# Chunk states and carried parts of a bidirectional scan as plain fp32 products, with the states in two buffers

## The chip, the cores and the metric

The kernel runs on one core of one Trainium2 chip. The metric is the device time of one execution in microseconds (us). Before the change three runs gave 1725.57 us as their median, between 1724.66 and 1726.45 us.

The engines have short names here: PE multiplies matrices (PEld is its loading of the stationary operand, which overlaps it), DVE is the vector engine, ACT the scalar engine, POOL is GpSimd, and SP issues most of the transfers (DMAs).

## What is computed

The kernel is one encoder layer over 1024 tokens of width 1024: a projection, a bidirectional state-space scan beside a neighbourhood attention, an output projection and an MLP. All inputs and outputs are fp32. The change touches the scan alone. For each direction it runs over 8 chunks of 128 tokens and 2 groups of 8 heads:

```python
    cb = jnp.einsum("bclgn,bcsgn->bclsg", cc, bc)
    y_diag = jnp.einsum("bclsge,bcsgep->bclgep", cb[..., None] * decay, xc)
    decay_to_end = jnp.exp(a_cum[:, :, -1:] - a_cum)
    chunk_states = jnp.einsum("bclgn,bclgep->bcgepn", bc, xc * decay_to_end[..., None])
    chunk_decay = jnp.exp(a_cum[:, :, -1])

    def step(h, inp):
        s_c, d_c = inp
        return d_c[..., None, None] * h + s_c, h
    ...
    _, h_in = lax.scan(step, h0, (jnp.moveaxis(chunk_states, 1, 0), jnp.moveaxis(chunk_decay, 1, 0)))
    h_in = jnp.moveaxis(h_in, 0, 1)
    y_off = jnp.einsum("bclgn,bcgepn->bclgep", cc, h_in) * jnp.exp(a_cum)[..., None]
    return (y_diag + y_off).reshape(bsz, t, SSM_GROUPS, HEADS_PER_GROUP, SSM_HEAD_DIM)
```

`chunk_states` (what a chunk adds to the state) and `y_off` (what the state carried into a chunk adds to its output) are the two products that are changed.

## The kernel before

**Split operands.** Nearly every large product of the kernel is made of fp32 operands split in two: a high part, the operand rounded to the type fp32r (an ACT copy), and a low part, the operand less its high part (a subtraction on DVE or POOL). The helper `mm3` (L178 to L180) issues three products of fp32r operands into one PSUM tile: high by high, high by low, low by high. The trace shows a product by its line in the helper and its tile.

**Stages.** The first part normalises and transposes the input, makes the scan's inputs (`xbc`, `conv`, `decays`) and the gate (`pz`). The scan follows (`backward` and `forward`, one chunk and one head group at a time, the two directions running against each other). Beside the scan runs the projection to q, k and v (`qkv_proj`, tiles `pq`, 1152 products), which needs nothing of the scan and fills PE between its steps. Then come the attention with the output projection, and the MLP.

**The scan's step.** For a direction d, a chunk c and a group g:

- `backward` multiplies B by C (tile `pcb`, L587), builds a 128x128 matrix for each head (`rb`: two POOL subtractions at L612, a DVE select at L618, an ACT exponential, a DVE product at L625), and multiplies each with the inputs `xs` (tile `pd`, L630, eight small products).
- `carried` makes the carried part: C is split (`ch` on ACT, L562; `cl` on DVE, L563), three products with the split state go to tile `py`, and a DVE product at L567 makes `yo` of it, which POOL adds to the output (`y1`, L641 or L666); DVE then adds `pd` (L642).
- `decay_state` makes the next state: POOL scales the inputs (`xw`, L653 or L672), `xw` is split (`xh` on ACT, L540; `xl` on DVE, L541), three products with the split B (`bNh`, `bNl`) go to tile `pS`. POOL multiplies the old state by its decay in place (`st`, L549), DVE adds `pS` (L550), and the new state is split (`sh` on ACT, L553; `sl` on DVE, L554) for the next `carried`. The first state of each direction and group is a DVE copy (L546).

There are 28 calls of `carried` and 28 of `decay_state`. The tiles `pcb`, `pS` and `py` share two PSUM buffers (tag "s"), so each has to wait until the last reader of the one two before it is done. B is split after a transpose in `conv`, four times (L184, L185).

**What sets the order.** The program is written once, step by step; a scheduler of the build then orders the instructions of each engine by its own estimate of the times, and each engine runs its list strictly in that order. A wait at the head of a list holds up everything behind it.

Of the kernel before, what the change touches and what calls it, by code (L numbers as in the profile page):

```python
# [9 lines left out]
F32 = mybir.dt.float32  # L10
F32R = mybir.dt.float32r
BF16 = mybir.dt.bfloat16
I32 = mybir.dt.int32
AF = mybir.ActivationFunctionType
# [4 lines left out]
P = 128  # L19
T = 1024  # L20
D = 1024
NT = T // P
# [33 lines left out]
def hymba_block(  # L56
# [25 lines left out]
    nc = tc.nc  # L82
    mul, add, sub = ALU.mult, ALU.add, ALU.subtract
# [25 lines left out]
    def ps_tp(name="tp"):  # L109
        return ps.tile([P, 512], F32, tag="tp", name=name, bufs=2)  # L110

    def ps_s(name="s"):
        return ps.tile([P, 512], F32, tag="s", name=name, bufs=2)
# [63 lines left out]
    def mm3(pt, ah, al, bh, bl, first, last):  # L177
        nc.tensor.matmul(pt, lhsT=ah, rhs=bh, start=first, stop=False)  # L178
        nc.tensor.matmul(pt, lhsT=ah, rhs=bl, start=False, stop=False)  # L179
        return nc.tensor.matmul(pt, lhsT=al, rhs=bh, start=False, stop=last)  # L180

    def split_from_psum(hi, lo, src, scalar=None):
        if scalar is None:
            nc.scalar.activation(hi, src, AF.Copy)  # L184
            nc.vector.tensor_tensor(lo, src, hi.bitcast(F32), op=sub)  # L185
        else:
            nc.scalar.activation(hi, src, AF.Copy, scale=scalar)
            nc.vector.scalar_tensor_tensor(
                lo, src, scalar, hi.bitcast(F32), op0=mul, op1=sub
            )  # L190
# [28 lines left out]
    with ExitStack() as ph:  # L219
# [4 lines left out]
        sp = ph.enter_context(tc.tile_pool(name="sp", bufs=1, side="right"))  # L224
        bT = sp.tile([P, 2, T], F32, name="bT")
        cT = sp.tile([P, 2, T], F32, name="cT")
        bNh = sp.tile([P, NT, 2, P], F32R, name="bNh")
        bNl = sp.tile([P, NT, 2, P], F32R, name="bNl")
        acum = sp.tile([P, 2, NT, 16], F32, name="acum")
        c1 = sp.tile([P, 2, NT, 16], F32, name="c1")  # L230
        e1 = sp.tile([P, 2, NT, 16], F32, name="e1")
# [6 lines left out]
        with ExitStack() as p0:  # L238
# [12 lines left out]
            for t in range(NT):  # L251
# [4 lines left out]
                for h in range(2):  # L256
                    s = slice(h * 512, (h + 1) * 512)
# [19 lines left out]
            for h in range(2):  # L277
                s = slice(4 * h, 4 * h + 4)
# [32 lines left out]
        with ExitStack() as p1:  # L311
            qp = p1.enter_context(tc.tile_pool(name="qp", bufs=2, side="right", reuse_waits="tile"))

            rrow = qp.tile([P, T], F32, name="rrow", bufs=1)
            for h in range(2):
# [5 lines left out]
                    op=mul,  # L321
# [127 lines left out]
            def conv(ft, ub):  # L449
                def tap(k):  # L450
                    return pcol[:, k * 12 + ft : k * 12 + ft + 1]

                acc = qp.tile([P, T], F32, tag="acc", name="acc")
                nc.scalar.activation(
                    acc,
                    ub[:, 0:T],
                    AF.Identity,
                    bias=pcol[:, 60 + ft : 61 + ft],
                    scale=tap(0),
                )  # L460
                for k in range(1, 5):
                    nc.vector.scalar_tensor_tensor(
                        acc, ub[:, k : k + T], tap(k), acc, op0=mul, op1=add
                    )
                dst = acc if ft < 8 else (bT, cT)[(ft - 8) // 2][:, ft % 2, :]
                nc.scalar.activation(dst, acc, AF.Silu)
                if ft >= 10:
                    return
                xn = qp.tile([P, NT, P], F32, tag="xn", name="xn") if ft < 8 else None
                for g in range(2):  # L470
                    pt = ps_tp("ptx")
                    for j in range(4):
                        c = 4 * g + j
                        nc.tensor.transpose(
                            pt[:, j * P : (j + 1) * P],
                            dst[:, c * P : (c + 1) * P],
                            ident,
                        )
                    pv = pt.rearrange("p (j f) -> p j f", j=4)
                    if ft < 8:  # L480
                        nc.scalar.copy(xn[:, 4 * g : 4 * g + 4, :], pv)
                    else:
                        s = (slice(None), slice(4 * g, 4 * g + 4), ft - 8)
                        split_from_psum(bNh[s], bNl[s], pv)
                if ft < 8:
                    nc.sync.dma_start(
                        xs_dr[:, :, ft * P : (ft + 1) * P].rearrange("c p f -> p c f"),
                        xn,
                    )
# [11 lines left out]
            for g in range(2):  # L501
                get = load_w_nat(w_in[0], 0, KD, OFF_Z + 512 * g, nc.vector)
                for t in range(NT):
                    pt = ps_mm("pz")
                    for k in range(KD):
                        s = (slice(None), k, slice(t * P, (t + 1) * P))
# [5 lines left out]
        def hb(v):  # L512
            return v.unsqueeze(2).broadcast_to([P, 8, HD])

        def h8(v):
            return v.rearrange("p (e d) -> p e d", d=HD)

        with ExitStack() as p2:
            qp = p2.enter_context(tc.tile_pool(name="qs", bufs=2, side="right", reuse_waits="tile"))
# [13 lines left out]
            st = [[None, None], [None, None]]  # L533

            def decay_state(d, c, g, xw):
                prev = st[d][g]
                pS = ps_s("pS")
                xh = qp.tile([P, 512], F32R, tag="xh", name="xh", bufs=1)
                xl = qp.tile([P, 512], F32R, tag="xl", name="xl", bufs=1)
                nc.scalar.activation(xh, xw, AF.Copy)  # L540
                nc.vector.tensor_tensor(xl, xw, xh.bitcast(F32), op=sub)  # L541
                mm3(pS, bNh[:, c, g, :], bNl[:, c, g, :], xh, xl, True, True)
                new = prev and prev[0]
                if prev is None:
                    new = qp.tile([P, 512], F32, tag=f"st{d}{g}", name="st", bufs=1)
                    nc.vector.tensor_copy(new, pS)  # L546
                else:
                    dec = ed[:, d, c, 8 * g : 8 * g + 8]
                    nc.gpsimd.tensor_tensor(h8(new), h8(new), hb(dec), op=mul)  # L549
                    nc.vector.tensor_tensor(new, new, pS, op=add)  # L550
                sh = qp.tile([P, 512], F32R, tag=f"sh{g}", name="sh", bufs=1)
                sl = qp.tile([P, 512], F32R, tag=f"sl{g}", name="sl", bufs=1)
                nc.scalar.activation(sh, new, AF.Copy)  # L553
                nc.vector.tensor_tensor(sl, new, sh.bitcast(F32), op=sub)  # L554
                st[d][g] = (new, sh, sl)

            def carried(d, c, g):
                py = ps_s("py")
                ct = cT[:, g, c * P : (c + 1) * P]
                ch = qp.tile([P, P], F32R, tag="ch", name="ch", bufs=2)  # L560
                cl = qp.tile([P, P], F32R, tag="cl", name="cl", bufs=2)
                nc.scalar.activation(ch, ct, AF.Copy)  # L562
                nc.vector.tensor_tensor(cl, ct, ch.bitcast(F32), op=sub)  # L563
                mm3(py, ch, cl, *st[d][g][1:], True, True)
                yo = qp.tile([P, 512], F32, tag="yo", name="yo", bufs=1)
                e = e1[:, d, c, 8 * g : 8 * g + 8]
                nc.vector.tensor_tensor(h8(yo), h8(py), hb(e), op=mul)  # L567
                return yo
# [12 lines left out]
            def backward(c, g):  # L581
# [57 lines left out]
                if c < NT - 1:  # L639
                    yo = carried(1, c, g)  # L640
                    nc.gpsimd.tensor_tensor(y1, y1, yo, op=add)  # L641
# [9 lines left out]
                if c > 0:  # L651
                    xw = qp.tile([P, 512], F32, tag="xw", name="xw", bufs=1)
                    nc.gpsimd.tensor_tensor(h8(xw), h8(xs), hb(wd[:, 1, c, hs]), op=mul)  # L653
                    decay_state(1, c, g, xw)
# [55 lines left out]
            for g in range(2):  # L710
                ps4 = slice(4 * g, 4 * g + 4)
                for b, pt, rt in qkv_proj(OFF_Q, g):
                    hl = normed_split(pt, rt, pcol[:, 80:81])
                    s = slice(b * P, (b + 1) * P)
# [58 lines left out]
    with ExitStack() as ph:  # L773
# [292 lines left out]
        for t in (0, 4, 1, 5, 2, 6, 3, 7):  # L1066
            xt = x2[:, t, :]
            for h, get in enumerate((get0, get1)):
                pt = ps_mm("po")
                s = slice(t * P, (t + 1) * P)  # L1070
# [3 lines left out]
                d = xt[:, h * 512 : (h + 1) * 512]  # L1074
# [173 lines left out]
    with ExitStack() as ph:  # L1248
# [32 lines left out]
        for fb in range(4):  # L1281
# [18 lines left out]
            for i in ORD:  # L1300
# [14 lines left out]
                for t in range(4):  # L1315
                    pt = (X if i in (1, 6, 7, 4) else Y)[t]
                    ts = slice(t * P, t * P + P)
                    for u in range(2):
                        (ah, al), (wh, wl) = wa[u]
                        for a in range(2):  # L1320
                            s = slice(a * 512 + t * P, a * 512 + t * P + P)
                            d = slice(a * 512, a * 512 + 512)
# [6 lines left out]
                    d = acc[:, tt, dh * 512 : (dh + 1) * 512]  # L1329
# [47 lines left out]
```

## Time and profile before

| what | value |
|---|---|
| median of three runs | 1725.57 us (1724.66 to 1726.45) |
| the profiled execution's own time | 1725.33 us |
| its span, from the first to the last instruction | 1723.5 us |
| granted PE clock, mean | 0.98 |
| DVE, ACT and POOL, share of the span | 64%, 42%, 41% |
| matrix and vector instructions that are recorded | 20879 |

The profile comes from one execution. An engine's busy time is that of its own instructions, without waits. Products on PE are pipelined: a record lasts longer than the distance to the next one's start, so that a busy PE isn't a PE at its peak, and a product that is held up shows as a longer record. A plain fp32 product is recorded as two instructions with one weight load each. "Idle before, releaser" tells what the engine waited for, as inferred from semaphores. Times in a view are us from the span's start unless marked ns.

### The profile page before, as it was taken

What the parts mean: (1) busy time and instruction counts of PE and PEld (TensorE: products, weight loads), DVE (VectorE), ACT (ScalarE), POOL (GpSimd) and SP (SyncE); (2) the same over time, 40 slices, a digit from 0 to 9 for tenths busy, and PEclk for the clock granted to TensorE, in tenths of its full rate; (3) what the DMA queues carried; (4) which work ended last, traced back from release to release, by engine and by line L of the source; (5) the groups of instructions that cost most, each with busy time, mean ns of one, the idle gap of its engine ahead of it and who ended that gap; (6) DMA issues with size and microseconds to landing.
All of it is one profiled execution on the core that took longest, in us unless ns stands there. A gap on an engine that the chain in (4) does not pass through costs nothing. (4 is left out here: it accounts for less than half of the span.)

```text
span 1723.5 us, 20879 instructions
## 1 busy us (share of the span) xinstructions
PE 1636.0 (95%) x7461; PEld 1304.6 (76%) x7461; DVE 1106.3 (64%) x1687; ACT 726.5 (42%) x1189; POOL 705.6 (41%) x496
## 2 busy tenths in 40 slices
PE   6999999989888999999999988999999978999999
PEld 5788888777766777777767767788888866888887
DVE  5767214889787744778787776454343359787863
ACT  5434223434344434555565533454444443333330
POOL 4000004888778741221242242244444426555551
PEclk9999999999998999999999999999999989999999
DMA  8213338876675796754453141254344394644231
GB/s 200 62 37 104 89 98 242 210 195 207 213 206 161 234 311 199 240 150 138 132 183 123 56 159 49 73 190 153 134 159 147 125 349 149 201 141 166 92 110 73
DMA packets 178499, 269.75 MB, mean 157 GB/s; under 512 B 13963, under 2 KB 105051, under 8 KB 178395
## 3 DMA queue, kind: packets, MB, share of 16 engines
q1 hardware_dynamic: 135419, 231.18, 42.6%
q10 hardware_dynamic: 42976, 37.23, 7.1%
q8 instruction: 59, 0.97, 0.2%
q14 instruction: 45, 0.37, 0.1%
HBM read 185.21 MB, written 86.50 MB: 158 GB/s over the span
## 5 line engine op out<-in xcount | busy, mean ns | idle before, releaser
L760 POOL TENSOR_TENSOR wl<-wraw,wh 128x1024 fp32r<-128x1024 f32 x110 | 300.1, 2740 | 350.1 <-ACT wh L759 336.7
L745 PE MATMUL px<-wh,ahl 128*128 128x512 f32 x512 | 163.7, 397 | 9.8 <-ACT ahl L759 9.8
L759 ACT ACTIVATE wh<-wraw 128x1024 fp32r<-128x1024 f32 x110 | 115.7, 1054 | 127.4 <-issue 42.4
L179 PE MATMUL pq<-wl,hTh 128*128 128x512 f32 x384 | 153.1, 400 | 4.6 <-DVE wl L149 4.4
L745 PE MATMUL px<-h,wh 128*128 128x512 f32 x496 | 156.5, 396 | 0.0
L178 PE MATMUL pq<-wh,hTh 128*128 128x512 f32 x384 | 153.1, 401 | 1.9 <-ACT wh L148 1.2
L180 PE MATMUL pq<-wh,hTl 128*128 128x512 f32 x384 | 151.9, 396 | 0.0
L759 ACT ACTIVATE ahl<-ar 128x1024 fp32r<-128x1024 f32 x56 | 58.9, 1053 | 173.0 <-PE px L745 89.6
L760 DVE TENSOR_TENSOR ahl<-ar,ahl 128x1024 fp32r<-128x1024 f32 x56 | 107.3, 1917 | 37.4 <-ACT ahl L759 36.2
L745 PEld LDWEIGHTS px<-wh,ahl 128*128 128x128 f32 x512 | 97.3, 190 | 31.9 <-ACT ahl L759 10.2
L745 PEld LDWEIGHTS px<-h,wh 128*128 128x128 f32 x496 | 93.4, 189 | 22.4
L149 DVE TENSOR_TENSOR wl<-wraw,wh 128x1024 fp32r<-128x1024 f32 x40 | 55.0, 1376 | 83.3 <-ACT wh L148 82.7
L878 POOL TENSOR_TENSOR mb<-braw,nam 128x256 f32<-128x256 f32 (+1 forms) x48 | 41.0, 884 | 159.7 <-DVE nmx L936 123.4
L184 ACT ACTIVATE pth<-ptp 128x384 fp32r<-128x384 f32 (+1 forms) x128 | 58.4, 459 | 107.8 <-PE ptp L959 106.8
L745 PE MATMUL px<-wl,ahl 128*128 128x512 f32 x256 | 100.9, 394 | 0.0
L745 PE MATMUL px<-h,wl 128*128 128x512 f32 x248 | 98.1, 396 | 0.0
L179 PEld LDWEIGHTS pq<-wl,hTh 128*128 128x128 f32 x384 | 73.2, 191 | 22.1 <-DVE wl L149 7.9
L149 POOL TENSOR_TENSOR wl<-wraw,wh 128x1024 fp32r<-128x1024 f32 x18 | 43.8, 2446 | 110.5 <-ACT wh L148 84.3
L745 PE MATMUL pz<-wh,ahl 128*128 128x512 f32 x256 | 82.8, 400 | 6.5 <-DVE acc L1330 5.0
L178 PEld LDWEIGHTS pq<-wh,hTh 128*128 128x128 f32 x384 | 72.9, 190 | 18.2 <-ACT wh L148 2.5
L180 PEld LDWEIGHTS pq<-wh,hTl 128*128 128x128 f32 x384 | 73.2, 191 | 14.7
L612 POOL TENSOR_TENSOR rb<-rb,c 128x512 f32<-128x512 f32 x64 | 75.0, 1192 | 21.5 <-DMA rb<-cum_dr 18.7
(265 smaller groups left out, 4242.6 us busy)
## 6 DMA issues: line engine op xcount, KB each, us to landing
act_dr<-cq SPq DMA_DIRECT2D x56, 512.0 KB, 3.0
ar<-act_dr SPq DMA_DIRECT2D x56, 512.0 KB, 3.8
wraw<-in_w_in_dram SPq DMA_DIRECT2D x44, 512.0 KB, 4.0
rb<-cum_dr SPq DMA_DIRECT2D x32, 512.0 KB, 7.6
wraw<-in_w_mlp_in_dram SPq DMA_DIRECT2D x32, 512.0 KB, 4.7
wraw<-in_w_mlp_out_dram SPq DMA_DIRECT2D x32, 512.0 KB, 5.3
q_dr<-hl ACTq DMA_DIRECT2D x64, 128.0 KB, 3.2
k_dr<-hl ACTq DMA_DIRECT2D x16, 512.0 KB, 3.2
```

The costliest lines, as they stand in the source:

```text
L149: lo_eng.tensor_tensor(lo[:, 0:n], raw[:, 0:n], hi[:, 0:n].bitcast(F32), op=sub)
L178: nc.tensor.matmul(pt, lhsT=ah, rhs=bh, start=first, stop=False)
L179: nc.tensor.matmul(pt, lhsT=ah, rhs=bl, start=False, stop=False)
L180: return nc.tensor.matmul(pt, lhsT=al, rhs=bh, start=False, stop=last)
L184: nc.scalar.activation(hi, src, AF.Copy)
L612: nc.gpsimd.tensor_tensor(rb[:, d], rb[:, d], c1[:, d, c, h0 : h0 + 4].unsqueeze(2).broadcast_to([P, 4, P]), op=sub,)
L745: nc.tensor.matmul(pt, lhsT=a, rhs=b, start=f, stop=l, skip_group_check=True)
L759: nc.scalar.activation(hl[0], src, AF.Copy)
L760: eng.tensor_tensor(hl[1], src, hl[0].bitcast(F32), op=sub)
L878: nc.gpsimd.tensor_tensor(mb[:, s].rearrange("p (s r c) -> p s r c", r=16, c=8), v[:, a:b], nam[:, s].rearrange("p (s r c) -> p s r c", r= ...
```

## The change

The two products of a scan step become one plain fp32 product each, so that nothing of `xw`, of the state, of C and of B has to be split. B is kept once as fp32 (`bN`, four ACT copies in place of four splits). The state gets two buffers for each direction and group: POOL reads the old one and writes its decayed copy into the other, where DVE adds `pS`. The first state's copy moves from DVE to ACT.

```diff
@@ -224,8 +224,7 @@
         sp = ph.enter_context(tc.tile_pool(name="sp", bufs=1, side="right"))
         bT = sp.tile([P, 2, T], F32, name="bT")
         cT = sp.tile([P, 2, T], F32, name="cT")
-        bNh = sp.tile([P, NT, 2, P], F32R, name="bNh")
-        bNl = sp.tile([P, NT, 2, P], F32R, name="bNl")
+        bN = sp.tile([P, NT, 2, P], F32, name="bN")
         acum = sp.tile([P, 2, NT, 16], F32, name="acum")
         c1 = sp.tile([P, 2, NT, 16], F32, name="c1")
         e1 = sp.tile([P, 2, NT, 16], F32, name="e1")
@@ -481,7 +480,7 @@
                         nc.scalar.copy(xn[:, 4 * g : 4 * g + 4, :], pv)
                     else:
                         s = (slice(None), slice(4 * g, 4 * g + 4), ft - 8)
-                        split_from_psum(bNh[s], bNl[s], pv)
+                        nc.scalar.copy(bN[s], pv)
                 if ft < 8:
                     nc.sync.dma_start(
                         xs_dr[:, :, ft * P : (ft + 1) * P].rearrange("c p f -> p c f"),
@@ -535,33 +534,20 @@
             def decay_state(d, c, g, xw):
                 prev = st[d][g]
                 pS = ps_s("pS")
-                xh = qp.tile([P, 512], F32R, tag="xh", name="xh", bufs=1)
-                xl = qp.tile([P, 512], F32R, tag="xl", name="xl", bufs=1)
-                nc.scalar.activation(xh, xw, AF.Copy)
-                nc.vector.tensor_tensor(xl, xw, xh.bitcast(F32), op=sub)
-                mm3(pS, bNh[:, c, g, :], bNl[:, c, g, :], xh, xl, True, True)
-                new = prev and prev[0]
+                nc.tensor.matmul(pS, lhsT=bN[:, c, g, :], rhs=xw, start=True, stop=True)
+                new = qp.tile([P, 512], F32, tag=f"st{d}{g}", name="st", bufs=2)
                 if prev is None:
-                    new = qp.tile([P, 512], F32, tag=f"st{d}{g}", name="st", bufs=1)
-                    nc.vector.tensor_copy(new, pS)
+                    nc.scalar.copy(new, pS)
                 else:
                     dec = ed[:, d, c, 8 * g : 8 * g + 8]
-                    nc.gpsimd.tensor_tensor(h8(new), h8(new), hb(dec), op=mul)
+                    nc.gpsimd.tensor_tensor(h8(new), h8(prev), hb(dec), op=mul)
                     nc.vector.tensor_tensor(new, new, pS, op=add)
-                sh = qp.tile([P, 512], F32R, tag=f"sh{g}", name="sh", bufs=1)
-                sl = qp.tile([P, 512], F32R, tag=f"sl{g}", name="sl", bufs=1)
-                nc.scalar.activation(sh, new, AF.Copy)
-                nc.vector.tensor_tensor(sl, new, sh.bitcast(F32), op=sub)
-                st[d][g] = (new, sh, sl)
+                st[d][g] = new
 
             def carried(d, c, g):
                 py = ps_s("py")
                 ct = cT[:, g, c * P : (c + 1) * P]
-                ch = qp.tile([P, P], F32R, tag="ch", name="ch", bufs=2)
-                cl = qp.tile([P, P], F32R, tag="cl", name="cl", bufs=2)
-                nc.scalar.activation(ch, ct, AF.Copy)
-                nc.vector.tensor_tensor(cl, ct, ch.bitcast(F32), op=sub)
-                mm3(py, ch, cl, *st[d][g][1:], True, True)
+                nc.tensor.matmul(py, lhsT=ct, rhs=st[d][g], start=True, stop=True)
                 yo = qp.tile([P, 512], F32, tag="yo", name="yo", bufs=1)
                 e = e1[:, d, c, 8 * g : 8 * g + 8]
                 nc.vector.tensor_tensor(h8(yo), h8(py), hb(e), op=mul)
```

The order of all engines is planned anew. On PE, in the first half of the scan, this is a step where a chunk's small products, the state's products and the next carried part stand in a row before:

```order
L179 MATMUL pq<-wl,hTh 128x512
L630 MATMUL pd<-xs,rb 128x64 x8
L178 MATMUL pS<-xh,bNh 128x512
L179 MATMUL pS<-xl,bNh 128x512
L180 MATMUL pS<-xh,bNl 128x512
L178 MATMUL py<-sh,ch 128x512
L179 MATMUL py<-sl,ch 128x512
L180 MATMUL py<-sh,cl 128x512
L705 MATMUL ptq<-ident,qn 128x128 x8
L180 MATMUL pq<-wh,hTl 128x512
```

And the same step in the changed program:

```order
L180 MATMUL pq<-wh,hTl 128x512
L616 MATMUL pd<-xs,rb 128x64 x8
L537 MATMUL pS<-xw,bN 128x512
L550 MATMUL py<-st,cT 128x512
L691 MATMUL ptq<-ident,qn 128x128 x8
L178 MATMUL pq<-wh,hTh 128x512
```

Six products have become two, and the neighbours are the same: `pS` still stands right behind `pd`, and `py` right behind `pS`, ahead of eight transposes (`ptq`) and the next projection products.

On DVE, at the step that adds to the output tile `y_2522`, there stands before (`qn` and `hl` belong to the projection, `rb` to the next chunk's matrices):

```order
L567 TENSOR_TENSOR yo<-py,e_100 128x512
L563 TENSOR_TENSOR cl<-cT,ch 128x128
L554 TENSOR_TENSOR sl<-st,sh 128x512
L699 SCALAR_TENSOR_TENSOR qn<-pq,rcol,rq 128x512
L550 TENSOR_TENSOR st<-st,pS 128x512
L541 TENSOR_TENSOR xl<-xw,xh 128x512
L642 TENSOR_TENSOR y_2522<-y_2522,pd 128x512
L188 SCALAR_TENSOR_TENSOR hl<-ptq,pcol,hl 128x512
L618 COPY_PREDICATED rb<-lmask,rb 128x512
L567 TENSOR_TENSOR yo<-py,e_100 128x512
L563 TENSOR_TENSOR cl<-cT,ch 128x128
L554 TENSOR_TENSOR sl<-st,sh 128x512
```

And at the same step of the changed program, where the output tile is called `y_2327`:

```order
L553 TENSOR_TENSOR yo<-py,e_99 128x512
L149 TENSOR_TENSOR wl<-wraw,wh 128x1024
L685 SCALAR_TENSOR_TENSOR qn<-pq,rcol,rq 128x512
L544 TENSOR_TENSOR st<-st,pS 128x512
L188 SCALAR_TENSOR_TENSOR hl<-ptq,pcol,hl 128x512
L628 TENSOR_TENSOR y_2327<-y_2327,pd 128x512
L604 COPY_PREDICATED rb<-lmask,rb 128x512
L553 TENSOR_TENSOR yo<-py,e_99 128x512
```

The five splits (`cl`, `sl`, `xl`, `cl`, `sl`) are gone, and the last subtraction of a weight split (`wl`) has moved from ahead of `yo` to behind it. The rest stands in the same order.

On POOL, around the same step, there stands before (`rq` belongs to the projection):

```order
L638 TENSOR_TENSOR y_2522<-xs,cf 128x512
L672 TENSOR_TENSOR xw<-xs,wd 128x512
L201 TENSOR_SCALAR rq<-sq 128x8
L202 TENSOR_TENSOR rq<-rq,half 128x8
L641 TENSOR_TENSOR y_2522<-y_2522,yo 128x512
L549 TENSOR_TENSOR st<-st,ed 128x512
L612 TENSOR_TENSOR rb<-rb,c_99 128x512 x2
L653 TENSOR_TENSOR xw<-xs,wd 128x512
```

And in the changed program:

```order
L624 TENSOR_TENSOR y_2327<-xs,cf 128x512
L201 TENSOR_SCALAR rq<-sq 128x8
L202 TENSOR_TENSOR rq<-rq,half 128x8
L627 TENSOR_TENSOR y_2327<-y_2327,yo 128x512
L598 TENSOR_TENSOR rb<-rb,c_98 128x512 x2
L658 TENSOR_TENSOR xw<-xs,wd 128x512
L543 TENSOR_TENSOR st<-st,ed 128x512
```

The forward direction's scaling of the inputs (`xw`, L672 before and L658 now) has moved from ahead of the addition of `yo` to behind it and behind two subtractions on `rb`, and the decay of its state (`st`) stands right behind it. (L653 is the backward direction's `xw`.) The work is the same.

## The prediction

> **What bounds the kernel now.** I read the page's busy times first, then the busy time by stage, then PE's waits in the stage of the scan.
>
> ```profile
> span 1723.5 us, 20879 instructions
> PE 1636.0 (95%) x7461; PEld 1304.6 (76%) x7461; DVE 1106.3 (64%) x1687; ACT 726.5 (42%) x1189; POOL 705.6 (41%) x496
> ...
> core 0: us, PE busy (x) PEld busy (x) DVE busy (x) ACT busy (x) POOL busy (x), PEclk, DMA share, GB/s
> ...
> 268.80:604.00 335.20, 302.81 (x1450) 242.29 (x1449) 264.52 (x388) 134.59 (x241) 262.83 (x242) 0.98 0.74 213
> 604.00:670.00 66.00, 65.34 (x297) 52.84 (x297) 25.03 (x32) 20.64 (x30) 20.33 (x22) 1.00 0.77 250
> ```
>
> PE is the busiest engine by far, so a change is worth what it does to PE: to its work, and to its waits. The change lies in the second row by stage, 268.8 to 604, where the scan runs beside the projection; there DVE (264.5 of 335.2) and POOL (262.8) are nearly as busy as PE. From 604 to 670 the rest of the projection runs alone.
>
> A busy PE hides stalls, since a product that is held up is a longer record. So I count PE's work over 268.8 to 670, which holds the whole projection and the whole scan.
>
> ```profile
> L179 PE MATMUL pq<-wl,hTh 128*128 128x512 f32 x384 | 153.1, 400 | 4.6 <-DVE wl L149 4.4
> L178 PE MATMUL pq<-wh,hTh 128*128 128x512 f32 x384 | 153.1, 401 | 1.9 <-ACT wh L148 1.2 <-DVE hl L188 0.6
> L180 PE MATMUL pq<-wh,hTl 128*128 128x512 f32 x384 | 151.9, 396 | 0.0
> ...
> 609.94 0.39 PE L179 MATMUL pq<-wl,hTh 128*128 128x512 f32 x1
> 610.17 0.39 PE L180 MATMUL pq<-wh,hTl 128*128 128x512 f32 x1
> 610.39 0.39 PE L178 MATMUL pq<-wh,hTh 128*128 128x512 f32 x1
> 610.62 0.39 PE L179 MATMUL pq<-wl,hTh 128*128 128x512 f32 x1
> ...
> L178 PE MATMUL pS<-xh,bNh 128*128 128x512 f32 x28 | 12.3, 441 | 1.7 <-ACT rb L623 1.0 <-ACT xh L540 0.7
> L178 PE MATMUL py<-sh,ch 128*128 128x512 f32 x28 | 12.7, 455 | 3.8 <-DVE yo L567 2.5 <-DVE st L550 1.3
> L630 PE MATMUL pd<-xs,rb 128*128 128x64 f32 x256 | 32.3, 274 | 8.2 <-DVE rb L625 7.3 <-issue 0.9
> L587 PE MATMUL pcb<-cT,bT 128*128 128x128 f32 x32 | 7.2, 310 | 8.6 <-DVE yo L567 7.5 <-DVE st L550 1.1
> L705 PE MATMUL ptq<-ident,qn 128*128 128x128 f32 x128 | 21.4, 280 | 2.7 <-DVE qn L699 1.8 <-ACT sz L576 0.8
> ...
> 435.65 1.89 PE L630 MATMUL pd<-xs,rb 128*128 128x64 f32 x16
> 418.82 0.60 PE L705 MATMUL ptq<-ident,qn 128*128 128x128 f32 x4
> ```
>
> Where nothing holds it up, a product of split operands starts 0.227 us after the one before (three steps from 609.94 to 610.62). The 3 x 384 products of the projection take 1152 x 0.227 = 261.5 us, and `pS` and `py` with three lines of 28 each 168 x 0.227 = 38.1. Sixteen records of `pd` take 1.89 us, the last with its 0.27 us of length, so they stand (1.89 - 0.27)/15 = 0.108 apart: 256 of them 27.6 us. Four transposes take 0.60 with a last one of 0.28, so 0.107 apart: 128 of them 13.7, and the 32 records of `pcb`, of the same size, 3.4. The sum is 344.3 us of work in 401.2 us. **About 57 us are lost to waits**, and these are what the change can win back.
>
> ```profile
> PE pcb L587 <- DVE yo L567: 7.5, 4, 3.1
> PE pd L630 <- DVE rb L625: 7.3, 9, 1.3
> PE pq L179 <- DVE wl L149: 4.4, 5, 1.7
> PE py L178 <- DVE yo L567: 2.5, 2, 2.0
> PE ptq L705 <- DVE qn L699: 1.8, 5, 0.9
> PE py L179 <- DVE sl L554: 1.6, 2, 1.2
> PE py L178 <- DVE st L550: 1.3, 4, 0.5
> ```
>
> These are PE's waits in that stage (total, times, longest). The rows name DVE for 26.4 us, and the two stage rows leave PE (335.2 - 302.8) + (66.0 - 65.3) = 33.1 us idle, so DVE is named for 80%. Only `sl` among them is removed. The others are instructions that stay, but that come late because DVE runs its list in order and is busy 79% of the stage.
>
> **The change part by part.** First the product itself: 28 `pS` and 28 `py` of three products each become one plain fp32 product each. The trace has the same shape once, in the first part, on operands that were not split.
>
> ```profile
> 47.97 0.40 PE L180 MATMUL px<-hTh,wl 128*128 128x512 f32 x1
> 48.20 1.02 PE L324 MATMUL prr<-dg,cst 128*128 128x512 f32 x2
> 48.66 0.80 PE L178 MATMUL px<-hTh,wh 128*128 128x512 f32 x1
> 49.30 0.39 PE L179 MATMUL px<-hTl,wh 128*128 128x512 f32 x1
> ```
>
> The product `prr` is recorded as two. It starts at 48.20; the product behind it is held up (0.80 instead of 0.39 long), and the next but one starts at 49.30. Less one step of 0.227 for the product between, `prr` takes 49.30 - 0.23 - 48.20 = 0.87 us, against 3 x 0.227 = 0.68 of the three that it replaces. **PE's work grows by 0.19 x 56 = 10.7 us.** In a stream without waits this comes out whole; it is covered only where PE would have waited anyway.
>
> Then the splits that go:
>
> ```profile
> L554 DVE TENSOR_TENSOR sl<-st,sh 128x512 fp32r<-128x512 f32 x28 | 24.0, 856 | 0.1
> L541 DVE TENSOR_TENSOR xl<-xw,xh 128x512 fp32r<-128x512 f32 x28 | 23.1, 826 | 5.8 <-ACT xh L540 5.7
> L563 DVE TENSOR_TENSOR cl<-cT,ch 128x128 fp32r<-128x128 f32 x28 | 13.1, 473 | 0.0
> L540 ACT ACTIVATE xh<-xw 128x512 fp32r<-128x512 f32 x28 | 17.5, 626 | 34.7 <-PE pS L180 10.3 <-POOL xw L653 6.7 <-PE pq L180 5.2
> L553 ACT ACTIVATE sh<-st 128x512 fp32r<-128x512 f32 x28 | 17.4, 623 | 16.3 <-DVE st L550 9.7 <-DMA q_dr<-hl 4.2 <-PE ptq L705 1.5
> ```
>
> DVE loses 24.0 + 23.1 + 13.1 = 60.2 us of its 264.5 in the scan, ACT at least 34.9 of 134.6. ACT is half idle, and I value its part at nothing, but for latency: a new state reaches its product a copy (0.62) and a subtraction (0.86) earlier. What DVE's part is worth has no row of its own. Below, it is worth nothing if the waits are somebody else's; above, it is worth all of DVE's share of the loss, 0.8 x 57 = 45.6 us. Between them I go by how waiting in a line grows with the line's busy time over its idle time: before, 264.5 / 70.7 = 3.7; after, 204.3 of about 322 us, or 204.3 / 118 = 1.7, so about half. **I take half of 45.6, 22.8 us won back**; this is an estimate from those rows.
>
> The rest I put at nothing. The decay of the state now writes another buffer: its old wait, for `sl`, was short, and its new one is for products two steps back. Four subtractions on B leave DVE, ahead of the scan, and four first copies of the state move from DVE to ACT, each of them one instruction of a 128x512 tile like those above (under 0.9 us) on an engine that isn't the bound there. The forward `xw` moves back on POOL, behind the addition of `yo`; this I keep as a rival. After the scan the lists of work are the same, and I expect no difference there.
>
> The sum: the profiled execution took 1725.33 us (0.24 under the median of the runs), + 10.7 - 22.8 = **1713.2 us**.
>
> **A rule weighed.** The Trainium skill, on the page "Perfetto Trace Analysis", section "Engine Utilization", puts the array's output rate for fp32 in low and high parts at half. By that rule a plain fp32 product would take twice a single pass, an estimate of 0.45 us from our step, and be cheaper than the three. The row of `prr` disagrees: 0.87 us, nearly four passes, and the sum goes by the row.
>
> **The rivals.**
>
> *Two passes instead of four.* If `prr` was slow for a reason of its own place, the new products take 2 x 0.227 = 0.45, and PE's work falls by 0.23 x 56 = 12.9 us: 1725.3 - 12.9 - 22.8 = 1690. For it speaks only that `prr` is two records; against it that the product behind it was visibly held up. 4%.
>
> *All of DVE's waits go.* 1725.3 + 10.7 - 45.6 = 1690; or most of them, say 40: 1696. For it speaks that DVE is named for four fifths of the idle time, against it that DVE itself waits for others (below). 10%.
>
> *A draw.* Half of what I expect is won back, 11.4 us, and pays just for the slower product: 1725.3 + 10.7 - 11.4 = 1724.6. This is so if half of the waits that name DVE are really POOL's, behind which DVE stands (next rival). 16%.
>
> *POOL takes the place of DVE, and the kernel gets slower.* POOL's work is unchanged, and DVE already waits for it:
>
> ```profile
> DVE rb L618 <- POOL rb L612: 16.6, 15, 2.5
> DVE y L642 <- POOL y L641: 12.3, 6, 4.5
> ...
> POOL rb L612 <- DMA rb<-cum_dr: 18.7, 12, 3.5
> ```
>
> The place is POOL's list around the addition of `yo`: that addition waits for `yo`, which waits for the longer `py`, and behind it stand two subtractions for the next matrices and now the forward `xw`, for which `pS` waits on PE. If POOL sets the pace, nothing is won back and the longer products are paid: 1725.3 + 10.7 = 1736. It decides once POOL's busy time and its own waits fill the scan: 262.8 + 18.7 = 281.5 us, against PE's work in it, 335.2 - 57 + 10.7 = 289. That is close. Against it speaks that the steps of both engines overlap with a free choice of filler, and that POOL's own operations lengthen where DVE works beside them, which becomes rarer:
>
> ```profile
> L612 POOL TENSOR_TENSOR rb<-rb,c x64: 1029/1041/2064, 280.4 to 595.6; 128x512 f32<-128x512 f32 x64
> ```
>
> The median is 1041 ns, but single ones took 2064. 18%.
>
> The Trainium skill, "SBUF — State Buffer", section "SBUF: two separate sides", says that a DVE instruction with two SBUF inputs and a GpSimd one that reads SBUF exclude each other for a whole instruction. By that rule the 84 removed subtractions would no longer hold POOL up. The long tail of the row above fits it, and no row here shows which instruction held which.
>
> **How the numbers follow.** My forecast has 52%, with a range of its own from 1700 to 1721. Faster by over 0.2% (3.5 us, about what a measurement of this kernel can tell from no change) are the forecast, all of DVE's waits and the two passes: 66%. The draw is 16%, slower 18%. The range for 8 in 10 goes from 1696, which leaves out the two passes and half of the case above it, to 1732, which leaves out more than half of the slower case.
>
> **What would show it.** The new products should be 56 pairs of records, each pair 0.87 us where the next product follows; 0.45 would prove the two passes. PE's work over the projection and the scan should count 355 us, and its lost time fall from 57 to about 34. Waits for `yo`, `rb` and `wl` on DVE should about halve; DVE's busy time in the scan should fall by some 60 us. If PE waits for POOL's `xw` instead, or DVE's waits for POOL's `rb` and `y1` grow, the slower rival holds. The prediction is wrong in its bounds if the scan's stage is unchanged and the time moves elsewhere.

## The result, and the profile after

The changed kernel takes 1731.88 us (median of 19 runs, 1723.20 to 1735.20), the kernel before 1725.89 us on the same chips (19 runs, 1721.92 to 1730.57). The ratio is 1.0027, with a 95% interval from 1.0017 to 1.0038: **slower by 0.27%**, where faster by 0.7% was forecast. The profiled execution took 1734.43 us. In what follows differences of times are taken from ratios to the kernel before, times 1725.9 us; by this measure the change costs 4.7 us (the two medians lie 6.0 us apart).

The page of the changed kernel, its busy times:

```profile
span 1732.5 us, 20534 instructions
PE 1642.9 (95%) x7405; PEld 1294.2 (75%) x7405; DVE 1049.2 (61%) x1595; ACT 693.7 (40%) x1109; POOL 696.6 (40%) x496
```

Its busy times by stage, in the columns of before. The last of the scan's products `pd` now ends at 586 us instead of 602, so the first row holds it with a little of the projection's rest:

```profile
core 0: us, PE busy (x) PEld busy (x) DVE busy (x) ACT busy (x) POOL busy (x), PEclk, DMA share, GB/s
268.00:590.00 322.00, 295.42 (x1338) 220.35 (x1337) 206.43 (x295) 97.67 (x156) 248.78 (x239) 0.98 0.73 219
590.00:673.20 83.20, 76.74 (x347) 61.95 (x346) 26.23 (x35) 22.74 (x34) 26.64 (x26) 1.00 0.68 211
```

DVE has lost 58 us of its work, as it should. The first and the last of the projection's products, of the kernel before (the first two rows) and of the changed kernel, tell how long the stage takes (duration in ns, then first and last start):

```profile
L178 PE MATMUL pq<-wh,hTh x384: 387/389/775, 268.9 to 669.8; 128*128 128x512 f32 x192
L180 PE MATMUL pq<-wh,hTl x384: 387/389/774, 269.6 to 670.2; 128*128 128x512 f32 x192
...
L178 PE MATMUL pq<-wh,hTh x384: 387/389/799, 268.1 to 672.8; 128*128 128x512 f32 x192
L180 PE MATMUL pq<-wh,hTl x384: 387/389/798, 268.8 to 673.2; 128*128 128x512 f32 x192
```

Before, 401.3 us pass from 268.9 to 670.2; after, 405.1 from 268.1 to 673.2. PE's work in it was counted as 344.3 us, and with 10.7 more it is 355.0. So the lost time, which is all that isn't counted work, went **from 57.0 to 50.1 us**, and not to 34. The other 5 us by which the two profiled spans differ lie behind the stage, in the attention part, where both kernels have the same work to do (380.6 us from 671.3 to 1051.9 before, 386.2 us from 675.0 to 1061.2 after). The kernel before took 386.1 us there too when its scan was written in another order (e12 below), so I don't lay those 5 us to the change; with one profile of each kernel it stays open whether they come with a plan or with a single execution.

Not all of the lost time is idle time of PE. The same stage as one row, before and then after:

```profile
268.90:670.20 401.30, 368.25 (x1746) 295.21 (x1745) 289.51 (x419) 155.21 (x270) 283.36 (x264) 0.98 0.74 219
268.10:673.20 405.10, 372.06 (x1682) 282.20 (x1682) 232.64 (x329) 120.35 (x188) 275.42 (x264) 0.99 0.72 217
```

**PE is idle for 33.0 us before and for 33.0 after.** The 6.9 us that were won back are none of it: they lie within PE's busy time, where a product that is held up, or that runs at a lower granted clock, is a longer record.

PE's waits over the stage after the change, in the columns of before:

```profile
PE pcb L573 <- DVE yo L553: 9.2, 5, 4.5
PE ptq L691 <- DVE qn L685: 9.2, 8, 3.0
PE pq L178 <- ACT wh L148: 3.6, 2, 2.8
PE py L550 <- DVE st L544: 3.2, 3, 2.0
PE pq L179 <- DVE wl L149: 2.9, 7, 0.6
PE pS L537 <- DVE st L544: 1.1, 2, 0.8
PE pd L616 <- DVE rb L611: 1.1, 2, 0.7
...
PE py L550 <- DVE yo L553: 0.4, 1, 0.4
```

Some waits shrank as forecast: for `rb` from 7.3 to 1.1 us, for `wl` from 4.4 to 2.9, of `py` for `yo` from 2.5 to 0.4, for `sl` from 1.6 to nothing. Others grew by as much: `pcb` for `yo` from 7.5 to 9.2, `ptq` for `qn` from 1.8 to 9.2, the projection for `wh` from 1.2 to 3.6. The rows that name DVE sum to 27.1 us; before they summed to 28.1, of which the prediction shows 26.4. And DVE itself waits more, for POOL above all:

```profile
DVE rb L604 <- POOL rb L598: 48.4, 19, 8.1
DVE hl L188 <- ACT hl L187: 43.4, 18, 7.9
DVE qn L685 <- POOL rq L202: 40.9, 26, 4.3
...
POOL rb L598 <- DMA rb<-cum_dr: 26.3, 19, 4.8
```

The first of these was 16.6 us before, and the other two were

```profile
DVE hl L188 <- ACT hl L187: 31.9, 14, 4.7
...
DVE qn L699 <- POOL rq L202: 13.8, 17, 2.1
```

so that the three together went from 62.3 to 132.7 us, while DVE's work fell by 57 us over the stage. One place on the timeline of POOL, DVE and PE shows how such a wait is passed on (start, duration, engine, then in brackets the idle time before it and its releaser):

```profile
552.46 2.04 POOL L598 TENSOR_TENSOR rb<-rb,c 128x512 f32<-128x512 f32 x2 [4.84 <-DMA rb<-cum_dr]
...
554.53 1.77 DVE L604 COPY_PREDICATED rb<-lmask,rb 128x512 f32<-128x512 int32 x1 [5.27 <-POOL rb L598]
556.20 0.67 DVE L560 TENSOR_TENSOR y<-y,sz 128x512 f32<-128x512 f32 x1
556.80 0.68 DVE L553 TENSOR_TENSOR yo<-py,e 128x512 f32<-128x512 f32 x1
...
557.62 0.46 PE L573 MATMUL pcb<-cT,bT 128*128 128x128 f32 x2 [4.54 <-DVE yo L553]
```

A load of `rb` comes late, POOL waits for it, the DVE select waits for POOL, `yo` stands behind the select in DVE's list, and PE waits for `yo` to free a PSUM buffer. PE's row names DVE, which itself had stood idle for 5.27 us, until 554.53. During most of PE's wait, which began at 553.08, DVE was busy, but with what had been held up.

At this place more than the wait was lost. Right behind it the granted clock was 0.50 for 10.3 us (the first row), and products of the projection started 0.43 us apart and not 0.227:

```profile
558.20:568.50 10.30, 7.01 (x17) 4.36 (x18) 8.88 (x13) 6.53 (x10) 7.74 (x8) 0.50 0.60 159
...
565.21 0.63 PE L178 MATMUL pq<-wh,hTh 128*128 128x512 f32 x1
565.64 0.63 PE L179 MATMUL pq<-wl,hTh 128*128 128x512 f32 x1
566.06 0.63 PE L180 MATMUL pq<-wh,hTl 128*128 128x512 f32 x1
```

PE was busy for 7.01 us of the stretch, so up to half of that, 3.5 us, is lost to the clock (an estimate from these rows). That the wait brought the lower clock about is not shown: no run changes one without the other.

### The profile page after: what moved, and what is told of

It reads as the page before. It is cut to its first block, busy times and chain, and to the rows that moved or that the text cites. A ratio compares the mean times of both kernels' runs of the same rounds, so it can differ in the third digit from the quotient of the medians.

```text
span 1732.5 us, 20534 instructions
## 1 busy us (share of the span) xinstructions
PE 1642.9 (95%) x7405; PEld 1294.2 (75%) x7405; DVE 1049.2 (61%) x1595; ACT 693.7 (40%) x1109; POOL 696.6 (40%) x496
## 5 line engine op out<-in xcount | busy, mean ns | idle before, releaser
L178 PE MATMUL pq<-wh,hTh 128*128 128x512 f32 x384 | 157.5, 413 | 3.6 <-ACT wh L148 3.6
L180 PE MATMUL pq<-wh,hTl 128*128 128x512 f32 x384 | 155.8, 406 | 0.0
L178 PE MATMUL po<-wh,yh 128*128 128x512 f32 x192 | 80.8, 421 | 2.3 <-ACT yh L187 1.9
```

## The experiments

Theory P: PE pays the longer products, and its waits hardly shrink. Theories Q, POOL and L: loads or POOL's list set the scan's pace. Theory N: no single engine does; from e8 on it is put more widely, that what counts is how the newly planned order of all engines happens to fall. "Time" is the median; each ratio is to the kernel before, run on the same chip.

**e1, the states alone plain**, and **e2, the carried parts alone plain**. Each is one half of the change on the kernel before; e2 has the two state buffers, e1 has not.

```diff
 # e1
...
-                mm3(pS, bNh[:, c, g, :], bNl[:, c, g, :], xh, xl, True, True)
+                nc.tensor.matmul(pS, lhsT=bN[:, c, g, :], rhs=xw, start=True, stop=True)
 # e2
...
-                mm3(py, ch, cl, *st[d][g][1:], True, True)
+                nc.tensor.matmul(py, lhsT=ct, rhs=st[d][g], start=True, stop=True)
```

> The kernel before with the product of the states alone made plain (pS from bN and xw; the carried parts stay split, the state stays in one buffer). It adds 28 x 0.19 = 5.3 us to PE and takes 23 us of DVE (xl) and 17.5 us of ACT (xh). Theory P (PE pays the longer products in full, and the waits hardly shrink): 1727 to 1731, lost time in the projection and scan 52 to 57 us. Theory Q (loads and POOL set the scan's pace, PE's own work does not matter): 1722 to 1726.

> The kernel before with the carried product alone made plain, with two buffers for a state (pS stays a product of split operands). It adds 5.3 us to PE and takes 37 us of DVE (sl, cl) and 26 us of ACT. Theory P: 1727 to 1731, as the states alone, the two together giving the change's +6. Theory Q: under 1726, and the waits of DVE for POOL's rb grow towards the changed kernel's 48 us.

Measured: e1 1726.47 us, ratio 1.0003 (0.9990 to 1.0016); e2 1724.38, ratio 0.9982 (0.9968 to 0.9996). The halves give +0.5 and -3.1 us where the whole gives +4.7. They do not add up, which neither P nor Q can say. Taken singly, e1 lies between the two ranges, with 55.0 us lost (404.6 us of stage less 349.6 of work) as P gave; e2 lies in Q's range, and DVE's waits for POOL's `rb` grew to 36.5 us in it, as Q gave.

**e3, one pass: the price of PE's work.** Each plain product is replaced by one fp32r product of the high parts; the low parts are left out.

```diff
-                nc.tensor.matmul(pS, lhsT=bN[:, c, g, :], rhs=xw, start=True, stop=True)
+                xh = qp.tile([P, 512], F32R, tag="xh", name="xh", bufs=1)
+                nc.scalar.activation(xh, xw, AF.Copy)
+                nc.tensor.matmul(pS, lhsT=bN[:, c, g, :], rhs=xh, start=True, stop=True)
...
-                nc.tensor.matmul(py, lhsT=ct, rhs=st[d][g], start=True, stop=True)
+                nc.tensor.matmul(py, lhsT=ch, rhs=st[d][g][1], start=True, stop=True)
```

> The changed kernel with one product of the fp32r high parts in place of each plain one: the low parts of all four operands are left out, ACT makes the high parts (43 us of ACT come back), DVE's work is that of the changed kernel. PE's work falls by 56 x 0.64 = 36 us against the changed kernel. Theory P: about 1732 - 36 = 1696, or at most a third of that lost again, up to 1708. Theory Q: PE waits instead, 1715 to 1728, and the scan ends no earlier than at 590 us.

Measured: 1709.09 us, ratio 0.9888 (0.9871 to 0.9905), which is 24.0 us under the changed kernel (1.0027 - 0.9888). Of 36 us taken from PE, two thirds come out. That lies just outside what theory P gave (1708) and well under theory Q's 1715. PE's work counts, though not whole.

**e4, one buffer for a state.**

```diff
-                new = qp.tile([P, 512], F32, tag=f"st{d}{g}", name="st", bufs=2)
+                new = prev
...
```

> The changed kernel with one buffer for a state, decayed in place as before. POOL's decay then has to wait for the carried product on PE that reads the state. Theory P and theory Q alike give the second buffer little: 1730 to 1736. If the two buffers are what changed POOL's order and so the waits, the time goes back towards 1726.

Measured: 1730.72 us, ratio 1.0028 (1.0016 to 1.0040), as the changed kernel. The second buffer is worth nothing that can be told in this order.

**e5, e6, e7: relieving POOL, and loading `rb` ahead.** On the changed kernel, e5 moves the decay and `xw` from POOL to DVE, e6 gives `rb` four buffers, e7 does both.

```diff
 # e5, e7
-                    nc.gpsimd.tensor_tensor(h8(new), h8(prev), hb(dec), op=mul)
+                    nc.vector.tensor_tensor(h8(new), h8(prev), hb(dec), op=mul)
-                    nc.gpsimd.tensor_tensor(h8(xw), h8(xs), hb(wd[:, 1, c, hs]), op=mul)
+                    nc.vector.tensor_tensor(h8(xw), h8(xs), hb(wd[:, 1, c, hs]), op=mul)
...
 # e6, e7
-                    rb = qp.tile([P, 2, 4, P], F32, tag="rb", name="rb", bufs=2)
+                    rb = qp.tile([P, 2, 4, P], F32, tag="rb", name="rb", bufs=4)
```

> The changed kernel with the decay of the states and the scaling of the inputs (xw) on DVE instead of POOL: 52 instructions, 54 us of POOL's 249 us in the scan, which take DVE about 52 x 0.7 = 36 us. Theory POOL (POOL's list sets the scan's pace, and PE's waits behind DVE are POOL's): lost time falls from 50 to under 40 us, 1715 to 1722. Theory L (the loads of rb behind the SP list set it): POOL waits for rb instead, 1728 to 1733. Theory N (the loss comes from the fixed order of several engines and no single one sets it): within 3 us of the changed kernel, and other waits take the place.

> The changed kernel with four buffers in place of two for rb, so that its loads can be issued two steps ahead. Theory L: POOL's wait for rb (26 us) falls under 10 us, the lost time by 10 us or more: 1718 to 1724. Theory POOL: a part of that, 1725 to 1731, since POOL's own work stays. Theory N: within 3 us of the changed kernel.

> Both together: POOL relieved by 54 us and rb loaded ahead. If POOL's list, by its work and its loads, is what PE waits for through DVE, the lost time falls to 25 to 35 us and the time to 1705 to 1718. If only the order matters (theory N), 1727 to 1735.

Measured: e5 1716.17 us, ratio 0.9942 (0.9924 to 0.9960); e6 1725.19, 0.9995 (0.9983 to 1.0008); e7 1726.01, 0.9995 (0.9980 to 1.0010). Against the changed kernel e5 gains 14.7 us, e6 5.5 and both together 5.5. The scan's row by stage of e5 shows POOL relieved:

```profile
268.00:590.00 322.00, 301.09 (x1368) 228.77 (x1367) 229.00 (x352) 98.75 (x158) 196.94 (x190) 0.97 0.74 221
```

e5 alone would settle it for theory POOL (197 us of POOL instead of 249, 38.2 us lost, and the time in its range). Theory N, which gave 3 us at most, is wrong for e5 and for e6. POOL's waits for the loads of `rb`, of e5, e6 and e7:

```profile
POOL rb L598 <- DMA rb<-cum_dr: 43.8, 22, 4.5
...
POOL rb L598 <- DMA rb<-cum_dr: 9.2, 8, 3.4
...
POOL rb L598 <- DMA rb<-cum_dr: 47.9, 24, 5.8
```

In the changed kernel it was 26.3. Part of what e5 took from POOL's work came back as waiting for the loads, as theory L said, though the time fell all the same. In e6 the wait fell under 10 us as theory L gave, but the lost time by 6 us and not by 10, and the time lies just above L's range. In e7 the four buffers did not shorten the wait. POOL has as little work in e7 as in e5 (190 and 197 us) and waits about as long, and yet e7 is 9 us slower; its time lies between the ranges of theory POOL and of theory N.

**e8 and e9: the dose.** The decay alone on DVE, and `xw` alone.

> The changed kernel with the decay of the states alone on DVE: 26 us less of POOL, about 17 more of DVE. Together with the next run it grades the dose of the relief that gave 1716. Theory POOL: about half of that gain, 1722 to 1726. Theory N (what counts is how the newly planned order happens to fall): no relation to the dose, anywhere from 1716 to 1735.

> The changed kernel with the scaling of the inputs (xw) alone on DVE: 30 us less of POOL, about 19 more of DVE. Theory POOL: about half of the gain, 1721 to 1726. Theory N: anywhere from 1716 to 1735.

Measured: e8 1731.83 us, ratio 1.0035 (1.0019 to 1.0051); e9 1728.17, 1.0015 (1.0004 to 1.0027). The halves of e5 gain -1.4 and 2.1 us, their sum nothing like 14.7. That speaks against theory POOL. Theory N's range of 1716 to 1735 could hardly be missed, so that it gains little by holding.

**e10 and e11: the same work in another order.** The two calls in the scan's loop change places, in the changed kernel and in the kernel before.

```diff
-                    backward(NT - 1 - i, g)
-                    forward(i, g)
+                    forward(i, g)
+                    backward(NT - 1 - i, g)
```

> The changed kernel with the forward step written ahead of the backward one in the scan's loop: the same instructions on every engine, in another planned order. It measures what an order alone is worth. Theory P and theory POOL: within 4 us of the changed kernel, 1728 to 1736. Theory N: it may differ by 5 us or more either way.

> The same swap in the kernel before. Theory P and theory POOL: within 4 us of the kernel before, 1722 to 1730. Theory N: 5 us or more either way. If the swapped pair differs by 4 to 8 us as the unswapped one does, the change's loss is its own and not the luck of one order.

Measured: e10 1730.21 us, ratio 1.0026 (1.0015 to 1.0036); e11 1738.46, ratio 1.0076 (1.0056 to 1.0096). The kernel before gets 13 us slower by an edit that changes no work, and in this order **the change is a gain of 8.6 us**. The first and last of the projection's products again, of e11 and then of e10, to compare with the four rows above:

```profile
L178 PE MATMUL pq<-wh,hTh x384: 387/389/795, 267.7 to 682.6; 128*128 128x512 f32 x192
L180 PE MATMUL pq<-wh,hTl x384: 387/389/628, 268.4 to 683.1; 128*128 128x512 f32 x192
```

```profile
L178 PE MATMUL pq<-wh,hTh x384: 387/389/798, 266.2 to 676.5; 128*128 128x512 f32 x192
L180 PE MATMUL pq<-wh,hTl x384: 387/389/799, 266.8 to 676.9; 128*128 128x512 f32 x192
```

In e11 the stage takes 415.4 us and loses 71.1, in e10 410.8 and 55.8. None of the difference to the unswapped pair is work, but it isn't all waiting either. The stage as one row, of e11 and of e10:

```profile
267.70:683.10 415.40, 375.50 (x1749) 300.99 (x1748) 290.44 (x419) 154.93 (x270) 287.25 (x264) 0.96 0.71 212
266.20:676.90 410.70, 379.66 (x1684) 290.79 (x1683) 228.43 (x329) 119.85 (x188) 267.23 (x264) 0.95 0.72 214
```

Of the 14.1 us that e11 loses more than the kernel before, 6.9 are idle time of PE (39.9 against 33.0). The others lie in its busy time, at a granted clock of 0.96 where it was 0.98. In e10 PE is even idle for 2 us less than in the changed kernel, with the clock at 0.95 where it was 0.99.

**e12 to e15: two more orders.** In e12 and e13 both backward steps of a pair of chunks are written ahead of both forward steps, in e14 and e15 behind them.

```diff
 # e12, e13 (e14, e15 with the two loops in the other order)
                 for g in range(2):
                     backward(NT - 1 - i, g)
+                for g in range(2):
                     forward(i, g)
```

> The kernel before with the two backward steps of a pair of chunks written ahead of its two forward steps: the same work in a third planned order. Theory N: differs from 1725.6 by 3 to 15 us, either way. Theory P: 1722 to 1730.

> The changed kernel in that third order. Theory P (the change's own cost is what the original order showed): 4 to 8 us over its partner e12. Theory N (that cost is luck of the order): the difference to e12 has another size or sign, as in the swapped pair, where the changed kernel was 8 us faster.

> The kernel before with the two forward steps of a pair written ahead of the two backward ones: a fourth planned order. Theory N: differs from 1725.6 by 3 to 15 us, either way. Theory P: 1722 to 1730.

> The changed kernel in that fourth order. Theory P: 4 to 8 us over its partner e14. Theory N: another size or sign. Over the four pairs, theory N gives a mean difference whose spread includes nought.

Measured, with the four orders side by side. "Lost" is read from the same two rows of each profile as above, less 344.3 us or 355.0 us of work:

| order | before: time, ratio | lost | changed: time, ratio | lost | change, us |
|---|---|---|---|---|---|
| as written | 1725.89, 1 | 57.0 | 1731.88, 1.0027 | 50.1 | +4.7 |
| swapped (e11, e10) | 1738.46, 1.0076 | 71.1 | 1730.21, 1.0026 | 55.8 | -8.6 |
| apart (e12, e13) | 1729.86, 1.0025 | 56.2 | 1727.03, 1.0009 | 43.2 | -2.8 |
| apart, forward first (e14, e15) | 1733.24, 1.0044 | 70.5 | 1729.01, 1.0020 | 49.9 | -4.1 |

The mean of the four changes is -2.7 us with a standard error of 2.8 (their spread of 5.5 over the root of four): no loss of its own can be told, and no sure gain. The kernel before is at its best in the order in which it was written; the changed kernel's four ratios lie within 0.2% of each other. Each "lost" is read from one profiled execution, and single ones of a kernel differ by several us, so that the column is rougher than the times. Of the forecasts, that for e10 came out as theory P had it, that for e12 fits both theories, and those for e11, e13, e14 and e15 fit theory N alone.

**e16, e17, e18: price and relief in other orders.** e16 is e3 in the order "apart", e17 is e5 in that order, e18 is e5 swapped.

> The one-pass kernel of e3 (the low parts of all four operands left out) in the third order, to be held against e13 (1727.0, lost time 43 us in its profile). If PE's work is paid at about two thirds in any order, as 23 of 36 us in the first order: 1701 to 1706, with 50 to 58 us lost. If that share was luck of the order: outside 1696 to 1711.

> The kernel of e5 (decay and xw on DVE) in the third order, to be held against e13 (1727.0). If relieving POOL by 54 us is worth 15 us by itself: 1710 to 1715. If e5 was a lucky order: 1722 to 1732.

> The kernel of e5 in the second order, to be held against e10 (1730.2). If relieving POOL is worth 15 us by itself: 1713 to 1718. If e5 was a lucky order: 1725 to 1735.

Measured: e16 1704.75 us, ratio 0.9877 (0.9859 to 0.9895), 22.8 us under its partner e13, where e3 gave 24.0: the price holds in the time. The profile fits less well: the stage of e16 takes 383.2 us and so loses 64 us where 50 to 58 were expected, and is 15.0 us shorter than that of e13, where e3's was 28.5 us shorter than the changed kernel's. Both kernels are planned anew, so two prices that agree do not exclude an order's luck in each. e17 1723.47, ratio 0.9986 (0.9972 to 1.0000), 4.0 us under e13; e18 1732.06, ratio 1.0034 (1.0021 to 1.0047), 1.4 us over e10. The relief that gave 14.7 us in one order gives 4.0 and -1.4 in two others, 5.8 us in the mean with a spread as large. e5 remains the fastest kernel here that leaves nothing out, 0.58% under the kernel before, but most of that goes with its order and doesn't carry over.

## Why the prediction was wrong

**The price of the product was right.** The rows of the changed kernel around one product of the states:

```profile
548.61 0.40 PE L178 MATMUL pq<-wh,hTh 128*128 128x512 f32 x1
548.85 1.02 PE L537 MATMUL pS<-xw,bN 128*128 128x512 f32 x2
549.31 0.80 PE L179 MATMUL pq<-wl,hTh 128*128 128x512 f32 x1
549.94 0.39 PE L180 MATMUL pq<-wh,hTl 128*128 128x512 f32 x1
```

549.94 - 0.23 - 548.85 = 0.86 us, as the row of `prr` had it (0.87). The rival of two passes is out. Of a microsecond of such work about two thirds reach the time (e3, e16). By that share the 10.7 us cost about 7, an estimate; that the prediction booked them whole was then an error of some 4 us on the cautious side.

**The term that failed is "I take half of 45.6, 22.8 us won back".** Measured in the profiles of the four orders, the change wins back 6.9, 15.3, 13.0 and 20.6 us, 14 in the mean and 6.9 in the one order that was to be predicted. DVE did lose its 58 us, and its share of the scan fell from 79% to 64%. But I took the waits that name DVE for waits behind DVE's work, and let half of them go with that work. They did not: PE's idle time stayed at 33.0 us, and the rows that name DVE went from 28.1 to 27.1. Much of it was a wait behind an instruction of DVE that itself came late from a wait for POOL, ACT or a load, and the time that DVE gained went into those waits (48.4 us for POOL's `rb`, where it was 16.6). This can be seen before the change too. Here is the chain of the place above in the kernel before, at one of the longest waits that the prediction booked to DVE:

```profile
516.09 2.04 POOL L612 TENSOR_TENSOR rb<-rb,c 128x512 f32<-128x512 f32 x2 [2.75 <-DMA rb<-cum_dr]
...
518.17 1.80 DVE L618 COPY_PREDICATED rb<-lmask,rb 128x512 f32<-128x512 int32 x1 [1.98 <-POOL rb L612]
...
521.30 0.68 DVE L567 TENSOR_TENSOR yo<-py,e 128x512 f32<-128x512 f32 x1
...
522.13 0.77 PE L587 MATMUL pcb<-cT,bT 128*128 128x128 f32 x2 [2.62 <-DVE yo L567]
```

The chain is shown in these two places; that it holds for most of the waits is read from the totals. The prediction quoted the rows that say so, as the case for a rival, and did not take them off the 45.6. It also carried DVE's share of PE's idle time, 33 us, over to all of the 57, though 24 of these lie in PE's busy time.

**What it left out altogether is the order.** The text ahead of it shows lists in which most neighbours stay neighbours, and the prediction goes on as if the new lists were the old ones less the removed rows. Even in the excerpt of DVE's list that isn't so: `hl` stands behind the addition of `pd` before (L642), and ahead of it after (L628). The lists are planned anew, and one plan against another is worth up to 13 us for the same work (e11). A forecast of 12 us for one particular pair of plans could not be sure of its sign; the range, whose upper end lies 0.1 us above the measured median, held only because of the rival that ended slower.

**The rivals.** POOL taking DVE's place had the right sign. Of the signs given for it, DVE's wait for POOL's `rb` grew, but that for `y1` didn't (12.3 us before, 11.1 after), and PE waited for `xw` for 0.4 us alone. Its mechanism is not shown: with POOL relieved by a fifth, the time fell by 14.7 us in one order, by 4.0 in another and not in a third (e5, e17, e18), and not by dose (e8, e9). No run shows a single engine that sets the scan's pace. In the mean of the four orders the change is worth -2.7 us, which is nearest to the draw (-0.7). Of the parts put at nothing, the second buffer was worth nothing that e4 can tell; the first copies and the split of B were not tried apart.

**What stays open.** Why the kernel before is 4 to 13 us better in its own order than in the three others wasn't found: the waits that differ lie on many pairs of instructions, and the granted clock of the stage differs with them, which no run tried apart. The four buffers for `rb` were tried in one order only, so whether their 5.5 us are the loads' or the order's is not known. Nor was one order tried with both kinds of product, since the build plans it anew with every edit; the four pairs stand in its place.

## What to carry to other kernels

Where a scheduler plans every engine's list anew, measure what an order alone is worth, by an edit that changes no work, before a change of half a percent is explained by its parts; compare the two versions in several orders. A wait that names an engine does not say that less work on that engine shortens it, even where the engine is busy during the wait: follow the row back to what that engine itself last waited for. Work on the busiest engine had a steady price here (two thirds of it in both orders tried), while time freed on its neighbours was not a sure gain. Look at the granted clock of a stage, too, before all that it loses is called waiting.

## What the runs showed of the hardware

A plain fp32 product of a 128x512 tile takes 0.86 to 0.87 us at full granted clock in two places, 3.8 times the 0.227 us of an fp32r one, and so 0.19 us more than three of these. The half rate that the Trainium skill ("Perfetto Trace Analysis", section "Engine Utilization") gives for fp32 in low and high parts would be 0.45 us, an estimate from our step. The product as a whole takes nearly twice that, and the measurement decides; each of its two records, half of 0.87 us, comes near it.

With the 84 DVE subtractions gone, POOL's own subtractions on `rb` became shorter, 1130 ns in the mean (L598, after) where they took 1192 (L612, before), while the shortest and the median hardly differ (1036 and 1042 ns after, 1029 and 1041 before). The longest fell from 2064 to 1635 ns:

```profile
L598 POOL TENSOR_TENSOR rb<-rb,c x64: 1036/1042/1635, 279.4 to 580.2; 128x512 f32<-128x512 f32 x64
...
L598 POOL TENSOR_TENSOR rb<-rb,c 128x512 f32<-128x512 f32 x64 | 70.9, 1130 | 26.4 <-DMA rb<-cum_dr 26.3
```

```profile
L612 POOL TENSOR_TENSOR rb<-rb,c 128x512 f32<-128x512 f32 x64 | 75.0, 1192 | 21.5 <-DMA rb<-cum_dr 18.7
```

That fits the exclusion of DVE and GpSimd which the prediction cites from the Trainium skill's page "SBUF — State Buffer"; no run here tried it alone.
